# Attention weights read back from DRAM by groups of 32 partitions: one change to a hybrid encoder block

## The chip, the cores and the metric

The kernel runs on one core of a Trainium2 chip. The metric is the device time of one execution in microseconds (us). Three runs of the kernel before took 1124.34, 1127.92 and 1130.77 us; their median is 1127.92 us.

## The reference

One encoder layer on 512 tokens of width 1024, in float32. It has a half-step feed-forward block, a mixer, and a second half-step feed-forward block. The mixer runs two branches on one normalised input and merges them with two sigmoid gates. Branch A is a convolution with two gated linear recurrences. Branch B, which the change touches, is neighbourhood attention over a grid of 8 rows and 64 columns with 16 heads of width 64:

```
x = x + 1/2 * SwiGLU_1(RMSNorm(x))
h = RMSNorm(x);  xr, gr, q, k, v, ga, gb = split(h @ W_in)
A = (rglru_forward(conv(xr)) + rglru_backward(conv(xr))) * gelu(gr)
q, k = RMSNorm per head
s = q . k over an 8 x 16 window + bias[head, drow, dcol]
B = softmax(s) @ v
x = x + (sigmoid(ga) * A + sigmoid(gb) * B) @ W_out
x = x + 1/2 * SwiGLU_2(RMSNorm(x))
```

## The kernel before

**Matmuls.** Every float32 matmul on weights is made of three: each operand is split into a high and a low part (`split`, ScalarE writes the high part, VectorE the low part), and high x high, high x low and low x high are summed. The weights of one chunk (`wraw`, 512 KB) are loaded by SyncE's queue, split into `wh` and `wl`, and used by 24 matmuls over 512 tokens. There are three `wraw` buffers and four pairs `wh`, `wl`, so the split of a later chunk waits until TensorE is done with an earlier one.

**Attention.** The 16 heads are handled in two halves (`hf` 0 and 1) of four head pairs each (`fi` 0 to 3; a pair is two heads of 64 on 128 partitions). The 512 tokens are in four column blocks `n` of 128 queries; a pair of column blocks is `n2`. In the first half TensorE turns q and k; in the second VectorE turns them in 32 x 32 blocks, and they go through DRAM (`qd`, `xqk`). For each head pair:

- `start` makes the high and low parts of q and k (`qh`, `ql`, `kh`, `kl`; lines 944 to 969).
- `scores` multiplies q and k (line 988), and makes the softmax: `so` adds the bias `bm` and takes the minimum of the negated sum on VectorE (line 1008), ScalarE makes the exponentials `p` (line 1015), VectorE the reciprocal `rs` (1017), ScalarE scales `p` (1020).
- `ship` turns the weights. With queries on partitions, `p` holds keys in columns. VectorE transposes 32 x 32 blocks into `pt` (lines 1029 and 1030), SyncE's queue stores `pt` to DRAM (`pd`, line 1032), and four loads by GpSimd's queue bring it back as `PT` with keys on partitions (line 1036). A PT has 128 partitions of four groups `j` of 896 bytes; group `j` holds the queries of one 32-partition block of `pt`.
- `apply` multiplies v by `PT` (line 1051) and ScalarE evicts it to `att` (1061). It reads all of a `PT`.

There are 16 such blocks, two for each head pair, called PT 1 to PT 16 here. `PT` has five buffers, `pd` four, `pt` two.

**Order.** The heads are written as generators and woven into the gate matmuls (`gates`, line 1113; matmuls at lines 172 to 174, eviction at line 1119): after a number of gate matmuls that a table of rates sets, one more step of the attention is written. `apply` of a head pair is written two pairs behind its scores in the second half (`ATT_LAG`), the last two at the end. A scheduler then orders each engine's instructions by its own estimates, and inserts the waits. Each engine runs its instructions in that order.

**GpSimd's queue** issues, one after the other: the four loads of each PT, the biases `bm` (line 895), and v in the shapes that the column blocks need (`vs`, line 872; `va` and `ve`, line 883, read only by `apply`). The kernel is built with `dynamic_dma_scratch_size=2048`, the room for what GpSimd writes to have its DMAs carried out.

Of the kernel before, what the change touches and what calls it, by code (L numbers as in the profile page):

```python
# [91 lines left out]
def block_kernel(ctx: ExitStack, tc, a, out):  # L92
    nc = tc.nc
# [14 lines left out]
    def nm(s):  # L108
        uid[0] += 1
        return f"{s}_{uid[0]}"  # L110
# [147 lines left out]
    def sub(out_, in0, in1, neg=False):  # L258

        if neg:  # L260
            nc.vector.scalar_tensor_tensor(out_, in0, -1.0, in1, ALU.mult, ALU.subtract)
        else:
            nc.vector.tensor_tensor(out_, in0, in1, ALU.subtract)
# [672 lines left out]
    def heads(hf, raws, qd):  # L936
# [86 lines left out]
        def ship(fi, n2):  # L1023

            outer, inner = soft.pop((fi, n2))
            t = big.tile([P, NCB, 7, 32], F32, tag="pt", bufs=2, name=nm("pt"))
            sub = lambda b, n: b[:, : n * P].rearrange("p (q c i) -> p q c i", q=n, i=32)
            to = t.rearrange("p c q i -> p q c i")
            nc.vector.transpose(to[:, 4:], sub(outer, 3))
            nc.vector.transpose(to[:, :4], sub(inner, 4))  # L1030
            d = dram.tile([P, NCB, 7 * 32], F32, tag="pd", bufs=4, name=nm("pd"))
            nc.sync.dma_start(d, t.rearrange("p c q i -> p c (q i)"))
            PT = big.tile([P, NCB, 7, 32], F32, tag="PT", bufs=5, name=nm("PT"))
            for j in range(4):
                q = slice(j * 32, (j + 1) * 32)
                nc.gpsimd.dma_start(PT[:, j].rearrange("p q i -> p (q i)"), d[q].rearrange("i c x -> c i x"))  # L1036
            PTs[fi, n2] = PT.rearrange("p a q i -> p q a i")

        def apply(fi, behind=None):
# [31 lines left out]
        for i, (fi, n2s) in enumerate(units):  # L1071
            behind = scores(fi, n2s)
            if i >= LC and 1 in units[i - LC][1]:
                apply(units[i - LC][0], behind)
            for n2 in n2s:
                ship(fi, n2)
            if 0 in n2s:
                if fi < 3:
                    start(fi + 1)
                if hf * 4 + fi + 1 < KT:  # L1080
                    bias(hf * 4 + fi + 1)
            if phase[0] == "g":
                yield
                if hf == 1:
                    yield
            yield
# [170 lines left out]
```

## Time and profile before

| | |
|---|---|
| median of three runs | 1127.92 us |
| profiled execution | 1128.13 us, span 1126.4 us |
| TensorE busy | 1100.3 us, 98% of the span |
| VectorE, ScalarE, GpSimd busy | 796.3, 619.5, 148.4 us |
| packets of GpSimd's DMA queue | 20752, 46.80 MB |
| PT loads | 64 of 112 KB, median 4.9 us from issue to landing |

Times in the trace are counted from the start of the span. Engines: PE is TensorE, DVE VectorE, ACT ScalarE, POOL GpSimd, SP SyncE. A row of the timeline gives start, duration, engine, line, operation, names out<-in, and in brackets the idle time before it with what ended it. "issue" means that the engine waited for nothing that the profile shows. Buffer numbers are left out of names in the profile and kept in the order listings.

### The profile page before, as it was taken

How to read it: one execution, taken by the hardware profiler on the slowest of the kernel's cores; microseconds unless marked ns; L12 is line 12 of the kernel's file. 1: busy time of each engine (PE TensorE's matmuls, PEld its weight loads, DVE VectorE, ACT ScalarE, POOL GpSimd, SP SyncE). 2: the span in 40 equal slices, each digit the busy share in tenths (PEclk: the TensorE clock that was granted, in tenths of full speed). 3: DMA queues.
4: the chain of work that ended last, by engine and by line, in shares of the span. 5: the costliest groups of instructions: out<-in, count | busy, mean ns of one | idle time of the engine just before them, and what ended most of it. 6: DMA issues, size and time to landing. Idle time of an engine off the chain costs nothing.

```text
span 1126.4 us, 17668 instructions
## 1 busy us (share of the span) xinstructions
PE 1100.3 (98%) x6779; PEld 974.1 (86%) x6779; DVE 796.3 (71%) x1228; ACT 619.5 (55%) x950; POOL 148.4 (13%) x243
## 2 busy tenths in 40 slices
PE   9999999999999999999999598999999999999998
PEld 8899999988888778787887476888999999998887
DVE  7877777785836877998875562768877877784642
ACT  8554545553624778877777462446645454464330
POOL 0000000000000441241234531000000000000000
PEclk9999999999999999999999799999999999999999
DMA  7566666643423784754798674377666666663321
GB/s 264 153 165 153 168 147 155 173 138 98 131 80 103 199 239 137 200 175 131 259 275 210 190 193 123 94 225 186 174 164 168 152 147 157 165 168 94 130 76 38
DMA packets 73571, 180.12 MB, mean 160 GB/s; under 512 B 23056, under 2 KB 26896, under 8 KB 73488
## 3 DMA queue, kind: packets, MB, share of 16 engines
q1 hardware_dynamic: 52160, 131.94, 36.4%
q0 software_dynamic: 20752, 46.80, 20.8%
q8 instruction: 53, 0.87, 0.3%
q10 hardware_dynamic: 576, 0.26, 0.1%
q14 instruction: 30, 0.25, 0.1%
HBM read 152.63 MB, written 17.83 MB: 151 GB/s over the span
## 4 chain that ended last, share of the span: by engine, by line
PE 90%; issue 3%; DMA 2%; POOL 2%; ACT 1%; DVE 1%; SPq 0%; POOLq 0%; ACTq 0%; DVEq 0%
PE acc L312 31%; PE acc L172 9%; PE acc L173 9%; PE acc L174 9%; PE aux L312 5%; PE acc L834 4%; PE acc L835 4%; PE acc L836 4%; PE aux L172 4%; PE aux L173 4%; PE aux L174 4%; POOL PT L1036 1%; DMA PT<-pd 1%; PE aux L742 1%; PE aux L1051 1%
## 5 line engine op out<-in xcount | busy, mean ns | idle before, releaser
L145 ACT ACTIVATE wh<-wraw 128x1024 fp32r<-128x1024 f32 (+3 forms) x236 | 233.4, 991 | 321.0 <-issue 88.5
L148 DVE TENSOR_TENSOR wl<-wraw,wh 128x1024 fp32r<-128x1024 f32 (+3 forms) x236 | 267.5, 1136 | 99.9 <-ACT wh L145 96.4
L312 PE MATMUL acc<-s,wh 128*128 128x256 f32 x1280 | 232.2, 283 | 0.0
L312 PEld LDWEIGHTS acc<-s,wh 128*128 128x128 f32 x1280 | 199.7, 192 | 0.0
L312 PE MATMUL acc<-s,wl 128*128 128x256 f32 x640 | 181.1, 283 | 0.0
L312 PEld LDWEIGHTS acc<-s,wl 128*128 128x128 f32 x640 | 122.9, 192 | 0.0
L172 PE MATMUL acc<-xh,wh 128*128 128x512 f32 x272 | 107.8, 396 | 0.0
L174 PE MATMUL acc<-xh,wl 128*128 128x512 f32 x272 | 106.5, 392 | 0.0
L173 PE MATMUL acc<-xl,wh 128*128 128x512 f32 x272 | 106.2, 391 | 0.0
L312 PE MATMUL acc<-xh,wl 128*128 128x256 f32 x320 | 90.6, 283 | 0.0
L312 PE MATMUL acc<-xl,wh 128*128 128x256 f32 x320 | 90.6, 283 | 0.0
L312 PE MATMUL acc<-xh,wh 128*128 128x256 f32 x320 | 90.5, 283 | 0.0
L834 PE MATMUL acc<-wh,xh 128*128 128x512 f32 x192 | 75.7, 394 | 1.0 <-ACT qk L846 1.0
L148 DVE TENSOR_TENSOR hl<-h,hh 128x512 fp32r<-128x512 f32 x88 | 57.3, 686 | 25.4 <-PE aux L173 24.3
L835 PE MATMUL acc<-wh,xl 128*128 128x512 f32 x192 | 74.8, 389 | 0.0
L836 PE MATMUL acc<-wl,xh 128*128 128x512 f32 x192 | 74.7, 389 | 0.0
L172 PE MATMUL aux<-hh,wh 128*128 128x512 f32 (+1 forms) x181 | 69.9, 386 | 0.0
L173 PE MATMUL aux<-hl,wh 128*128 128x512 f32 (+1 forms) x181 | 69.9, 386 | 0.0
L174 PE MATMUL aux<-hh,wl 128*128 128x512 f32 (+1 forms) x181 | 69.9, 386 | 0.0
L173 PE MATMUL acc<-hl,wh 128*128 128x512 f32 (+1 forms) x176 | 67.9, 386 | 0.0
L174 PE MATMUL acc<-hh,wl 128*128 128x512 f32 (+1 forms) x176 | 67.9, 386 | 0.0
L172 PE MATMUL acc<-hh,wh 128*128 128x512 f32 (+1 forms) x176 | 67.9, 386 | 0.0
(226 smaller groups left out, 2304.1 us busy)
## 6 DMA issues: line engine op xcount, KB each, us to landing
wraw<-wqkv SPq DMA_DIRECT2D x24, 512.0 KB
wraw<-wg SPq DMA_DIRECT2D x24, 512.0 KB
wraw<-w1d SPq DMA_DIRECT2D x22, 512.0 KB
wraw<-w2s SPq DMA_DIRECT2D x22, 512.0 KB
pair<-w2s SPq DMA_DIRECT2D x22, 512.0 KB
wraw<-w2d SPq DMA_DIRECT2D x22, 512.0 KB
wraw<-w1s SPq DMA_DIRECT2D x18, 512.0 KB
pair<-w1s SPq DMA_DIRECT2D x18, 512.0 KB
```

The costliest lines, as they stand in the source:

```text
L145: nc.scalar.activation(H, raw, AF.Copy)
L148: return nc.vector.tensor_tensor(L, raw, H.bitcast(F32), ALU.subtract)
L172: nc.tensor.matmul(ps, wh, xh, start=first, stop=False, skip_group_check=skip)
L173: nc.tensor.matmul(ps, wh, xl, start=False, stop=False, skip_group_check=skip)
L174: mark["mm"] = nc.tensor.matmul(ps, wl, xh, start=False, stop=last, skip_group_check=skip)
L312: mm = nc.tensor.matmul(o, w_[:, c], x_, start=first and m + k == 0 and w_ is H and x_ is xh_, stop=m + k == 4 and w_ is L, skip_group_che ...
L742: prev, mm = mm, nc.tensor.matmul(ps[d][b], W[w][o, c], X[x][o], start=x == 1, stop=w + x == 0)
L834: nc.tensor.matmul(pss[j], xh[kk][:, tj], H[:, s], start=kk == 0, stop=False)
L835: nc.tensor.matmul(pss[j], xl[kk][:, tj], H[:, s], start=False, stop=False)
L836: mark["mm"] = nc.tensor.matmul(pss[j], xh[kk][:, tj], L[:, s], start=False, stop=kk == KT - 1)
L1036: nc.gpsimd.dma_start(PT[:, j].rearrange("p q i -> p (q i)"), d[q].rearrange("i c x -> c i x"))
L1051: mm = nc.tensor.matmul(pv[h2 * HD : (h2 + 1) * HD, n * P : (n + 1) * P], vt[:, (fi * 2 + h2) * HD : (fi * 2 + h2 + 1) * HD], PT[:, q], st ...
```

## The change

The four loads of a PT are cut another way. Before, load `j` wrote group `j` of all 128 partitions, from 32 rows of `pd` that lie one behind the other. Now load `c` writes the 32 partitions of key block `c`, all four groups of them, from one 896-byte piece of each of the 128 rows of `pd`. The number of loads, their bytes and the length of the contiguous pieces are the same, and so is the data in `PT`.

```
             PT = big.tile([P, NCB, 7, 32], F32, tag="PT", bufs=5, name=nm("PT"))
-            for j in range(4):
-                q = slice(j * 32, (j + 1) * 32)
-                nc.gpsimd.dma_start(PT[:, j].rearrange("p q i -> p (q i)"), d[q].rearrange("i c x -> c i x"))
+            for c in range(4):
+                q = slice(c * 32, (c + 1) * 32)
+                nc.gpsimd.dma_start(PT[q].rearrange("p j q i -> p j (q i)"), d.rearrange("(j i) c x -> c i j x", j=4)[c])
             PTs[fi, n2] = PT.rearrange("p a q i -> p q a i")
```

In the built program a load's counts, from the outermost dimension, go from 128 x 1 x 224 on the tile's side and 4 x 32 x 224 in DRAM to 32 x 4 x 224 on both sides. The change applies to both halves of the heads. The scheduler's order moves as well, from about the second head pair of the second half on; the places that count are shown in the prediction.

## The prediction, made before the result was known

> **What bounds the kernel now.** I read the slices of the page first, then the idle times of TensorE in its timeline, then what the releasers of those waits waited for themselves.
>
> ```profile
> PE 1100.3 (98%) x6779; PEld 974.1 (86%) x6779; DVE 796.3 (71%) x1228; ACT 619.5 (55%) x950; POOL 148.4 (13%) x243
> PE   9999999999999999999999598999999999999998
> PEclk9999999999999999999999799999999999999999
> ```
>
> TensorE works without a break except in the 23rd and 25th slice, where the granted clock dips too; a slice is 28.2 us, so that is from about 620 us on, and by the timeline 606 to 696 us. Only this stretch has time to give. Its idle times in the timeline of PE (idle and releaser in brackets):
>
> ```profile
> 608.21 0.39 PE L988 MATMUL aux<-kl,qh 64*128 64x256 f32 x2 [1.47 <-DVE kl L965]
> 630.38 0.39 PE L988 MATMUL aux<-kl,qh 64*128 64x256 f32 x2 [4.52 <-DVE kl L965]
> 633.21 0.70 PE L1051 MATMUL aux<-PT,va 128*64 128x128 f32 x4 [0.43 <-DMA PT<-pd]
> 638.82 1.12 PE L1051 MATMUL aux<-PT,vs 128*64 128x128 f32 x8 [3.92 <-DMA PT<-pd]
> 641.75 0.69 PE L1051 MATMUL aux<-PT,va 128*64 128x128 f32 x2 [1.81 <-DMA va<-vd]
> 644.72 0.45 PE L1051 MATMUL aux<-PT,va 128*64 128x128 f32 x1 [2.29 <-DMA va<-vd]
> 664.24 0.66 PE L1051 MATMUL aux<-PT,vs 128*64 128x128 f32 x8 [1.71 <-DMA PT<-pd]
> 692.66 1.12 PE L1051 MATMUL aux<-PT,vs 128*64 128x128 f32 x8 [4.02 <-DMA PT<-pd]
> ```
>
> They add up to 20.2 us, 14.2 of it on transfers that POOL issues (PT, va). After the long ones the clock is halved for a while (windows: length, PE busy, ..., PEclk):
>
> ```profile
> 631.10:634.40 3.30, 2.87 (x30) 2.60 (x28) 3.30 (x14) 1.36 (x6) 1.02 (x2) 0.50 0.94 179
> 638.00:648.00 10.00, 5.09 (x38) 3.98 (x40) 0.49 (x1) 0.60 (x1) 7.10 (x10) 0.50 0.55 155
> 692.60:695.80 3.20, 3.14 (x19) 2.62 (x20) 0.00 (x0) 0.60 (x1) 0.00 (x0) 0.50 0.03 5
> ```
>
> 2.87 + 5.09 + 3.14 = 11.1 us of matmuls at half clock, of which half, 5.5 us, is lost. The stretch costs 25.7 us in all.
>
> Why the transfers are late stands in POOL's waits and its timeline:
>
> ```profile
> POOL PT L1036 <- issue: 64.7, 30, 6.3
> 526.66 2.03 POOL L1036 DMA_DIRECT2D PT<-pd  x3 [24.53 <-DMA pd<-pt]
> 530.60 0.66 POOL L1036 DMA_DIRECT2D PT<-pd  x1 [1.90 <-issue]
> 610.82 0.59 POOL L895 DMA_DIRECT2D bm<-rpb  x1
> 614.36 0.70 POOL L1036 DMA_DIRECT2D PT<-pd  x1 [2.94 <-issue]
> 618.55 0.66 POOL L1036 DMA_DIRECT2D PT<-pd  x1 [0.86 <-issue]
> 619.20 1.16 POOL L895 DMA_DIRECT2D bm<-rpb  x2
> 617.61 0.36 DVE L1008 CUSTOM_DVE_ANT_0 so<-aux,bm 128x192 f32<-128x192 f32 x1 [7.66 <-DMA bm<-rpb]
> DMA to landing us min/median/max: 3.6/4.9/10.5
> ```
>
> Each block needs four PT loads. Three go out back to back, and the fourth stalls in its own issue until the first has landed (526.66 + 3.6 = 530.3, issue at 530.60): three PT loads in flight fit somewhere, four don't. At 618.55 to 619.20 two bm loads, 128 rows each as well, pass with PT loads in flight and no stall. So a PT load takes much more of what is full. What it takes is seen where queue q0 carries three PT loads alone (packets and issues of 540 to 545.2 us):
>
> ```profile
> DMA packets 631, 1.25 MB, mean 241 GB/s; under 512 B 328, under 2 KB 337, under 8 KB 631
> q0 software_dynamic: 375, 0.33, 25.9%
> PT<-pd POOLq DMA_DIRECT2D x3, 112.0 KB, 4.4
> ```
>
> No row of a PT load is under 896 B, yet about 296 of q0's 375 packets are under 512 B (the other 32 of the 328 are completions of two transfers on q1). Per load that is 125 packets, near 16 rings of 8: 4 rings with 32 rows each (packets of five rows and one of two, the 9 between 512 B and 2 KB), 12 rings with padding of the same length, and a completion on each. I read: the rows go over 4 engines, and every ring is charged 32 entries and a completion, 33 in all. Three loads are 99; four would be 132.
>
> **The change part by part.** Issues, bytes and row size stay: 64 loads of 128 rows of 896 B. What changes is the pair of leading counts: 128 on the tile's side against 4 in DRAM before, 32 against 32 now. A bm load, 128 against 128, has no padding. By that row 32 against 32 spreads over 16 engines with 8 rows and a completion each, 9 entries; the other end is that it stays at 33. I take 9, since nothing in the new shape has a 4 in front. [...]
>
> Then four loads take 36 entries, POOL issues a block in 4 x 0.67 = 2.7 us, and what is queued behind (bm, va) goes out at once. The scheduler reorders as well, in three places that matter. POOL, between the last block of the first half (PT_6059) and the first two of the second (PT_6236, PT_6246):
>
> ```order
> +L1036 DMA PT_6059<-pd_6057 32x4x224 x4
>  L895 DMA bm_6266<-rpb 128x640
> -L1036 DMA PT_6059<-pd_6057 128x1x224 x4
>  L895 DMA bm_6462<-rpb 128x640
>  L895 DMA bm_6464<-rpb 128x640
> -L1036 DMA PT_6236<-pd_6234 128x1x224 x4
> +L1036 DMA PT_6236<-pd_6234 32x4x224 x4
> +L1036 DMA PT_6246<-pd_6244 32x4x224 x4
>  L879 MEMSET ve_6269 128x512
> ```
>
> bm_6266, for which DVE waited until 617.61, now stands behind a whole block of loads. DVE, ahead of the second head pair's softmax (so_6393):
>
> ```order
>  L965 TENSOR_TENSOR kl_6254<-xqk_6144,kh_6253 128x4x8x16
>  L148 TENSOR_TENSOR wl_6716<-wraw_6714,wh_6715 128x1024
> +L1119 TENSOR_TENSOR pair_6476<-acc_6478,rstd_3727 128x512
> +L148 TENSOR_TENSOR wl_6756<-wraw_6754,wh_6755 128x1024
>  L1008 ISA so_6393,nmx_6394<-aux_6361,bm_6264 128x192
> ```
>
> The softmax now waits for a gate chunk of 24 matmuls (acc_6478) that PE starts after the scores. And DVE, ahead of the third pair's scores, which need kl_6452:
>
> ```order
> -L148 TENSOR_TENSOR wl_6756<-wraw_6754,wh_6755 128x1024
> +L962 SCALAR_TENSOR_TENSOR ql_6450<-xqk_6259,gq_3677,qh_6449 128x4x128
> +L1119 TENSOR_TENSOR pair_6477<-acc_6542,rstd_3727 128x512
> +L148 TENSOR_TENSOR wl_6928<-wraw_6926,wh_6927 128x1024
> +L965 TENSOR_TENSOR kl_6452<-xqk_6259,kh_6451 128x4x8x16
>  L1017 RECIPROCAL rs_6360<-rs_6360 128x2
> ```
>
> kl_6452 moves ahead of the transposes, but behind the eviction of chunk acc_6542, all of whose 24 matmuls now precede the scores (21 before). The walk uses these rows:
>
> ```profile
> 609.89 0.50 PE L172 MATMUL acc<-xh,wh 128*128 128x512 f32 x1
> 625.47 0.39 PE L174 MATMUL acc<-xh,wl 128*128 128x512 f32 x1
> L148 DVE TENSOR_TENSOR wl<-wraw,wh 128x1024 fp32r<-128x1024 f32 x11 | 13.4, 1214 | 0.9 <-ACT wh L145 0.9
> L145 ACT ACTIVATE wh<-wraw 128x1024 fp32r<-128x1024 f32 x11 | 11.6, 1056 | 16.4 <-PE acc L173 15.1 <-DMA wraw<-wg 1.3
> L1119 DVE TENSOR_TENSOR pair<-acc,rstd 128x512 f32<-128x512 f32 x11 | 7.5, 684 | 32.3 <-PE acc L174 32.2
> L965 DVE TENSOR_TENSOR kl<-xqk,kh 128x512 fp32r<-128x512 f32 x3 | 2.0, 683 | 0.0
> 682.31 1.99 POOL L1036 DMA_DIRECT2D PT<-pd  x3 [3.59 <-DMA pd<-pt]
> 674.87 0.33 SPq L1032 DMA_DIRECT2D pd<-pt  x1
> ```
>
> First the scores at 608.21: they wait for an eviction and a kl after the last gate matmul, 0.68 + 0.68 and a hand-over, 1.47. Order and wait stay. From 609.89 to 625.47 there are 69 gate matmuls, 0.229 us apart, so a chunk of 24 lasts 5.5 us. Chunk acc_6478 ends near 615.5; the split of the next weights (1.06 on ACT, whose buffer that chunk frees, 1.21 on DVE) ends near 617.8, and the softmax starts there, as late as the 617.61 of now; bm_6266 has room if POOL no longer stalls. SP is reordered too: the store of this pair's first block (pd_6432) stands behind two weight loads whose buffer comes free with the split near 623.4, about when its transposes end; that costs 1 us at most, and the block is wanted 25 us later. Chunk acc_6542 ends at 609.89 + 72 x 0.229 + 0.2 = 626.5. Behind it come wh 1.06 on ACT, wl 1.21 and kl 0.68 on DVE with their hand-overs, 3.1 us, and the scores start at 629.6. This wait is 3.1 instead of 4.52. Is the clock halved behind it? The idle times of 1.71 and 1.47 were not followed by half clock, those of 3.92 and more were; 3.1 is nearer to 3.92, so I take one dip of 3.4 us, 1.7 lost, with 0 as the other end.
>
> From there: two applies (PV products) without a wait, 48 gate matmuls, then the fourth pair's scores. Their kl also stands behind an eviction now (kl_6672 behind that of acc_6753, whose last four matmuls move ahead of the scores): again 0.68 + 0.68, 1.47 us, where the kl was ready before. Then apply, 48 gates, apply, 36 gates, the last apply. The blocks have room: by my walk PT 12 lands about 5 us before its apply, PT 14 some 7. The tight one is PT 16. Its store went out at 674.87, 15 us after the scores, and took 7.4 us to 682.3. With the fourth scores at 648, softmax and transposes of 10 us (nothing between them waits for a chunk now), a store of 7.4, an issue of 2.7 and 4 us to land give 672; its first product is due near 674. I cost it at 0, with 4 us as the other end.
>
> **The sum.** Before: 20.2 + 5.5 = 25.7. After: 1.47 + 3.1 + 1.47 idle and 1.7 for the clock, 7.7. Gain 18.0. PE is busy without a break from 696 us to the end, so the gain reaches the end. The profiled execution took 1128.13 us with a span of 1126.4; the median of the runs is 1127.92. 1128.13 - 18.0 = 1110.1; I forecast **1110 us**. Its own range: 1108 without the clock dip, 1116 with PT 16 late by 4 us and a dip behind it.
>
> **The rivals.** *Late landings.* Each load now writes into 32 partitions only. If it then lands as late as the loads did in the busiest stretch (maximum 10.5, median 4.9), the tight block comes 5.6 - 2 = 3.6 us late, with another dip, 1.7, and one or two of the earlier waits stay in part, 2 to 4: 1110 + 7 to 9, about 1118. For it: 32 x 896 B x 4 in a quarter of the tile. Against: xqk loads of the same grouping hold up nobody on PE. [...]
>
> *The ring stays full, slower.* If a load still takes 33 entries (the scheduler keeps its new order all the same), bm_6266 stands behind the block whose fourth load went out at 618.55. It goes at 619.2 and lands with the bm median of 6.3 at 625.5, not 617.5:
>
> ```profile
> DMA to landing us min/median/max: 3.8/6.3/8.8
> ```
>
> The second softmax, kl_6452 and all behind slip by up to 8 us, of which 3 lie under the gates; the waits for PT stay. 1128 + 5 = 1133. 99 entries are seen to fit, so it cannot decide below 25 entries a load.
>
> *No change.* POOL's stall goes, but the blocks were late for another reason, the stores on SP and the chunk-locked DVE, and the waits come back elsewhere. Against: 64.7 us of POOL's idle time is its own issue, and block 16's store waited for nothing but its transposes. 1127.
>
> **How the numbers follow.** Relief as walked 0.67, late landings 0.17, no change 0.08, slower 0.08. A difference of 0.5%, 5.6 us, is about what a measurement tells from none. Faster 0.84, same 0.08, slower 0.08. The range for all, 1104 to 1119, takes in the first two cases and, below, a walk that overrates the two kl waits and the dip by most of their 6 us.
>
> **What would show it.** In the page, q0 falls from 20752 packets by 64 x (128 - 48) = 5120 to about 15632 (16 x 3 per load in place of 16 x 8). That settles the engines by itself. POOL's timeline shows PT x4 in one row, its waits on issue for PT fall from 64.7 to a few us, DVE's wait for bm is gone. PE keeps three idle times, near 1.5, 3.1 and 1.5 us, all for kl, and none for PT or va but perhaps the last; PEclk dips at most once. Wrong it would be if q0 keeps its packets, or if PE waits for kl for more than 8 us in all.
>
> ```profile
> q0 software_dynamic: 20752, 46.80, 20.8%
> ```

## The result, and the profile after

The changed kernel took 1109.04 us, the median of four runs (1108.49 to 1109.71), beside 1127.82 us for the kernel before in the same comparison (1124.34 to 1130.77, four runs). The ratio is 0.9835, with a 95% interval of 0.9806 to 0.9864, so 15 to 22 us were gained. The profiled execution took 1108.49 us with a span of 1106.7 us.

The page of the changed kernel, the rows that answer those of before (busy times, slices, clock, GpSimd's queue):

```profile
PE 1093.7 (99%) x6779; PEld 969.0 (88%) x6779; DVE 796.1 (72%) x1228; ACT 619.1 (56%) x950; POOL 140.1 (13%) x243
PE   9999999999999999999999899999999999999998
PEclk9999999999999999999999999999999999999999
q0 software_dynamic: 15632, 46.70, 21.5%
```

The hole in the 23rd and 25th slice is gone but for one 8, and so is the dip of the clock. The queue's packets are 15632, 48 a load in place of 128, to the packet the number forecast. The span fell by 19.7 us: 6.6 us of TensorE's busy time (1100.3 to 1093.7; 5.5 of them are the prediction's half clock, 5.7 by the exact windows of the last section; the rest is not traced) and 13.1 us of its idle time (1126.4 - 1100.3 = 26.1 before, 1106.7 - 1093.7 = 13.0 now). The waits left in the attention stretch, in TensorE's timeline:

```profile
559.54 0.44 PE L1051 MATMUL aux<-PT,va 128*64 128x128 f32 x4 [1.26 <-DVE ql L962]
609.56 0.38 PE L988 MATMUL aux<-kl,qh 64*128 64x256 f32 x2 [1.48 <-DVE kl L965]
630.63 0.38 PE L988 MATMUL aux<-kl,qh 64*128 64x256 f32 x2 [2.78 <-DVE kl L965]
648.61 0.39 PE L988 MATMUL aux<-kl,qh 64*128 64x256 f32 x2 [1.47 <-DVE kl L965]
```

No wait is on a transfer any more. Three are the predicted ones for `kl`; the first, 1.26 us, wasn't predicted. The profiled execution is the fastest of the four and has full clock throughout; the other three took 0.5 to 1.2 us more at a granted clock of 0.998 in place of 1.000. GpSimd's waits on its own issue (total, times, longest), two pieces of its timeline, and the landings of PT:

```profile
POOL va L883 <- issue: 12.1, 7, 3.3
POOL ve L883 <- issue: 6.2, 4, 2.0
POOL PT L1036 <- issue: 0.2, 1, 0.2
615.59 2.18 POOL L1036 DMA_DIRECT2D PT<-pd  x4 [6.07 <-DMA pd<-pt]
661.97 2.26 POOL L1036 DMA_DIRECT2D PT<-pd  x4 [1.22 <-DMA pd<-pt]
DMA to landing us min/median/max: 2.6/5.4/8.0
```

The 64.7 us of stalls on PT are 0.2. Four loads go out in one row; what GpSimd waits for ahead of them is the store (`pd<-pt`), not room. The median landing is 5.4 us, 4.9 before; the shortest is 2.6 instead of 3.6 and the longest 8.0 instead of 10.5. The medians are not like for like, as four loads are now in flight at once and before it was three.

### The profile page after: what moved, and what is told of

It reads as the page before. It is cut to its first block, busy times and chain, and to the rows that moved or that the text cites. A ratio compares the mean times of both kernels' runs of the same rounds, so it can differ in the third digit from the quotient of the medians.

```text
span 1106.7 us, 17673 instructions
## 1 busy us (share of the span) xinstructions
PE 1093.7 (99%) x6779; PEld 969.0 (88%) x6779; DVE 796.1 (72%) x1228; ACT 619.1 (56%) x950; POOL 140.1 (13%) x243
## 3 DMA queue, kind: packets, MB, share of 16 engines
q0 software_dynamic: 15632, 46.70, 21.5%
## 4 chain that ended last, share of the span: by engine, by line
PE 95%; DMA 1%; DVE 1%; ACT 1%; issue 1%; SPq 0%; ACTq 0%; DVEq 0%
PE acc L312 31%; PE acc L172 11%; PE acc L173 10%; PE acc L174 10%; PE aux L312 5%; PE acc L834 4%; PE aux L172 4%; PE aux L174 4%; PE aux L173 4%; PE acc L835 4%; PE acc L836 4%; PE aux L1051 1%; PE aux L742 1%; PE aux L988 1%; DMA vd<-v 1%
```

## The experiments

The rivals for the gain: room for entries in GpSimd's queue (the theory), the scheduler's new order, the narrow shape of 32 partitions, and the larger number of engines as such. Each comparison had its own runs of the kernel before, with medians of 1127.82 to 1130.07 us.

**The kernel before with more room, and with less.** The order of all engines stays as before.

```
-dynamic_dma_scratch_size=2048
+dynamic_dma_scratch_size=3072      (and 1024)
```

> The kernel before, with 3072 in place of 2048 bytes of scratch for GpSimd's DMAs, nothing else; every engine's order stays. Theory of the ring (a PT load takes 33 entries a ring, 2048 bytes hold 128 of them, so 3072 hold 192 and five loads fit): the fourth load of a block no longer stalls, PT x4 in one row of POOL's timeline, POOL's waits on issue for PT fall from 64.7 us to under 15, and most of the gain comes without the change: 1108 to 1116 us. Rival of the engines (the gain is that the rows go over 16 engines and land sooner): loads still on 4 engines, 1125 to 1130 us. Rival of the order (the gain is the scheduler's new order): 1125 to 1130 us.

> The kernel before, with 1024 bytes, same order. Theory of the ring: 64 entries, a second load of 33 never fits, so each PT load waits until the one before has landed: 64 x 4.9 us is 314 us of POOL's time in place of some 165 now (525 to 690 us), and va and ve go one at a time too. TensorE waits for blocks: 1220 to 1290 us. Rivals of the engines and of the order: 1125 to 1130 us.

With 3072 it took 1112.51 us (1108.82 to 1113.47), ratio 0.9859 (0.9836 to 0.9882). GpSimd's waits, the landings of PT and TensorE's waits for transfers in that kernel:

```profile
POOL PT L1036 <- issue: 15.4, 12, 3.5
DMA to landing us min/median/max: 3.5/6.0/11.3
630.50 0.43 PE L1051 MATMUL aux<-PT,va 128*64 128x128 f32 x2 [0.77 <-DMA va<-vd]
633.08 0.29 PE L1051 MATMUL aux<-PT,va 128*64 128x128 f32 x1 [2.14 <-DMA va<-vd]
674.82 0.66 PE L1051 MATMUL aux<-PT,vs 128*64 128x128 f32 x8 [1.21 <-DMA PT<-pd]
```

Room alone, without one changed load and in the old order, brings nearly all of the gain; its interval overlaps that of the change. The loads are cut there as before (20752 packets, by the prediction's reading over 4 engines), so neither more engines nor the new order are needed. The stalls on PT fell from 64.7 to 15.4 us, just over the 15 expected. The trace is of its execution of 1108.82 us, at a clock of 1.000.

With 1024 it took 1295.04 us (one run), 5 us above the range expected. TensorE's waits, and GpSimd's timeline at the first blocks:

```profile
PE aux L1051 <- DMA PT<-pd: 128.4, 11, 17.4
532.20 0.69 POOL L1036 DMA_DIRECT2D PT<-pd  x1 [2.10 <-issue]
538.22 0.69 POOL L1036 DMA_DIRECT2D PT<-pd  x1 [5.33 <-issue]
```

Each load goes out alone, after a wait of 2.10 and 5.33 us in its issue. What fits at 2048 can be bounded from the traces of the kernel before and of the changed one. Reckoned with 33 entries for an old PT load, a `va` or a `ve` and 9 for any other, up to 117 entries are in flight in the first and up to 126 in the second, the load just issued among them. Of the stalls over 0.2 us that GpSimd has on the issue of PT, `va` and `ve`, 35 of 38 and 10 of 11 begin where the next load would bring 132 or more. In proportion to the size this gives, as an estimate, 63 to 66 entries at 1024 and 189 to 198 at 3072: one old load fits, or five. The traces show them one at a time at 1024, three in a row at 2048 (526.66 us) and four in a row at 3072 (640.77 us). The 64, 128 and 192 of the expectations lie within these bounds; that the room is exactly this isn't shown.

**The changed kernel with less and with more room.** Same one-number edit, same order as the changed kernel.

> The changed kernel with 1024 bytes in place of 2048, order as changed. Theory of the ring: four PT loads take 36 of 64 entries and still go without a stall; va and ve (33 each) go one at a time, about 3 us apiece for 12 in each half, mostly hidden: 1109 to 1119 us, q0 at 15632 packets. If the new loads took 33 entries after all, over 1220 us.

> The changed kernel with dynamic_dma_scratch_size=3072, all engines in the same order. Nothing of the computation is left out. Theory (with 9 entries a load the ring no longer bounds anything that PE waits for): GpSimd's waits on issue for va and ve, 18 us together, fall to less than 4, and the time stays at 1108 to 1110 us. Rival (what is left of the stalls, va and ve with 33 entries each, still costs PE's time): 1104 to 1107 us.

With 1024 it took 1127.04 us (1124.24 to 1129.15), ratio 0.9985 (0.9972 to 0.9998), no gain left: a miss by 8 us at the least. GpSimd's waits and TensorE's two longest:

```profile
POOL PT L1036 <- issue: 7.0, 8, 2.8
POOL va L883 <- issue: 38.6, 13, 4.9
POOL ve L883 <- issue: 26.4, 8, 5.4
634.41 0.58 PE L988 MATMUL aux<-kl,qh 64*128 64x256 f32 x2 [6.90 <-DVE kl L965]
648.14 0.44 PE L1051 MATMUL aux<-PT,va 128*64 128x128 f32 x1 [7.65 <-DMA va<-vd]
```

The PT loads go out in fours or threes even there (three at 617.09 and at 621.58 us), with 7.0 us of stalls. The loads of v, `va` and `ve` (64 rows of 4 pieces each), still take 33 entries, by the same reckoning, and go one at a time (635.15, 639.68, 642.55, 645.45 and 648.31 us). I had expected that, and about its price in stalls (12 in each half at 3 us, 72 us; found 65.0); what I had wrong is "mostly hidden". They hold up all that is behind them, and TensorE waits 7.65 us for a `va` itself. The same room for entries, then, with another payer.

With 3072 it took 1109.40 us (1107.60 to 1109.61), ratio 0.9820 (0.9797 to 0.9843), the time of the changed kernel:

```profile
POOL ve L883 <- issue: 6.3, 3, 3.2
POOL va L883 <- issue: 0.4, 1, 0.4
```

The stalls of `va` and `ve` fall from 18.3 to 6.7 us (not below 4 as expected) and TensorE gains nothing: what is left of them at 2048 is off its path.

**Which half's loads.** The new loads in one half of the heads, the old ones in the other (`hf == 0`, then `hf == 1`).

```
+if hf == 0:            # hf == 1 in the second kernel
     for c in range(4): ...   # loads by 32 partitions
+else:
+    for j in range(4): ...   # loads by group j, as before
```

> The new loads for PT 1 to 8 alone; PT 9 to 16 are loaded by key block as before, and PE, DVE and SP keep the order of before. Nothing of the computation is left out. Theory (room for entries): q0 falls by half, to 20752 - 32 x 80 = 18192 packets. GpSimd's waits on issue for PT fall to about half of 64.7 us; the backlog of the first half is gone, so bm comes in time, DVE's wait of 7.66 us goes, and of PE's waits the 4.52 for kl and the clock dip behind it; the stalls of the second half stay and with them 1.7 + 4.0 us for PT and the dip of 1.6 behind 692 us. So half to two thirds of the gain of 18.8 us: 1116 to 1121 us. Rival (the new order makes the gain): no gain, about 1128 us. Second rival (the first half's stalls do no harm, since PE waited only after 606 us): 1126 to 1128 us.

> The new loads for PT 9 to 16 alone; PT 1 to 8 are loaded by key block as before, and PE and DVE have the order of the changed kernel. Nothing of the computation is left out. Theory (room for entries): 18192 packets on q0; the stalls around PT 7 and PT 8 stay (bm goes out late, 618 to 619 us, and kl is late with it, 4 to 5 us of PE's idle time with a clock dip of 1.7), PE waits for no PT after 650 us: 1113 to 1118 us. Rival (the new order makes the gain): 1109 us. Second rival (only the second half counts): 1109 to 1111 us. With this the gains of the two halves are to be compared: more than 19 us together means that either alone removes part of the same waits.

("By key block as before" in these two means the old loads, by group `j`.)

The first half alone: 1116.41 us (1115.38 to 1116.71), ratio 0.9878 (0.9858 to 0.9899), in the range expected. It has the order of before on TensorE and VectorE, so the order isn't what gains. Both kernels have 18192 packets. What it has left, GpSimd's waits and TensorE's timeline:

```profile
POOL PT L1041 <- issue: 32.2, 18, 5.7
633.57 0.29 PE L1056 MATMUL aux<-PT,va 128*64 128x128 f32 x1 [2.86 <-DMA va<-vd]
679.92 1.12 PE L1056 MATMUL aux<-PT,vs 128*64 128x128 f32 x8 [3.99 <-DMA PT<-pd]
```

The second half alone: 1121.55 us (1116.52 to 1122.36), ratio 0.9916 (0.9887 to 0.9946). That is slower than the 1113 to 1118 expected (one of its four executions, 1116.52, lies within), and the rival of the order, 1109, falls: this kernel has the new order on TensorE and VectorE and keeps less than half of the gain.

```profile
611.71 0.66 POOL L1041 DMA_DIRECT2D PT<-pd  x1 [6.83 <-issue]
635.24 0.69 PE L1056 MATMUL aux<-PT,va 128*64 128x128 f32 x4 [3.35 <-DMA PT<-pd]
640.26 1.12 PE L1056 MATMUL aux<-PT,vs 128*64 128x128 f32 x8 [3.05 <-DMA PT<-pd]
644.91 0.44 PE L1056 MATMUL aux<-PT,va 128*64 128x128 f32 x1 [2.64 <-DMA va<-vd]
```

The miss: I had charged the old loads of the first half with a late bias only. A single old load stalls for 6.83 us there, behind it the next blocks and `va` go out late, and the applies of 632 to 645 us wait for them; the clock is halved for 20.5 us, 629.7 to 650.1 by the spacing of the matmuls (mean granted clock 0.991 of 1120.6 us), in which some 11.2 us of matmuls ran, so that 5.6 us are lost. The half clock begins behind the wait of 2.78 us for `kl`, which the changed kernel has too; here TensorE was busy 0.6 us in the 3.41 us ahead of it. It lasts through the waits for PT and `va`. By the medians the backlog of the first half is the larger part of the loss. The gains, 13.7 and 8.5 us, add up to 22.2, more than the 18.8 of the whole change, but within their intervals; that both remove some of the same waits stays likely and unproved.

**Sixteen engines without the narrow shape.** The store is cut in four and laid out so that a load by group `j` reads 128 contiguous rows.

```
-d = dram.tile([P, NCB, 7 * 32], ...);  nc.sync.dma_start(d, t...)
+d = dram.tile([4, NCB, 32, 7 * 32], ...)
+for j in range(4):
+    nc.sync.dma_start(d[j].rearrange("c i x -> i c x"), t[j * 32 : (j + 1) * 32]...)
 for j in range(4):
-    nc.gpsimd.dma_start(PT[:, j]..., d[q].rearrange("i c x -> c i x"))
+    nc.gpsimd.dma_start(PT[:, j]..., d[j].rearrange("c i x -> (c i) x"))
```

> Loads by key group j of 128 partitions again, as in the kernel before, but the store to DRAM is cut in four on SyncE's queue and laid out so that the 128 rows of each load lie one behind the other: leading counts 128 on both sides, 16 engines, without the narrow shape of 32 partitions. Nothing of the computation is left out. The scheduler orders all engines anew with the three more stores a block. Theory (the number of engines and entries counts, not which partitions a load writes): q0 15632 packets, no stall of a fourth PT load, no wait of PE for PT, 1106 to 1114 us; the three more stores a block (4 instead of 1 on SyncE's queue) can cost up to 3 us. Rival (it is the grouping by 32 partitions that helps): waits for PT stay, 1122 to 1130 us.

It took 1118.60 us (1116.97 to 1118.94), ratio 0.9897 (0.9876 to 0.9918), outside both ranges. Its queue, GpSimd's wait for PT, TensorE's only long wait, and part of SyncE's queue there:

```profile
q0 software_dynamic: 15632, 46.70, 20.6%
POOL PT L1036 <- issue: 1.8, 8, 0.5
615.43 0.79 PE L172 MATMUL acc<-xh,wh 128*128 128x512 f32 x1 [12.98 <-ACT wh L145]
600.38 5.62 SPq L1033 DMA_DIRECT2D pd<-pt  x8
608.33 11.59 SPq L163 DMA_DIRECT2D wraw<-wg  x5
```

What the theory says of the loads holds: the packets, no stall, and no wait of TensorE for a PT. So the grouping by 32 partitions as such isn't what helps; a load that covers 128 partitions in 48 packets does too. The loads of that kernel also land sooner, 2.2 us at the least and 4.2 in the median, beside 2.6 and 5.4 for those of 32 partitions. The price of the stores was mis-sized. I had put 3 us on SyncE's queue, for more stores in it; what cost the time, by this trace, is the order that the scheduler gave that queue. Between 555 and 608 us it issues no load of gate weights, where the changed kernel issues seven; the last eight stores stand at 600.38 to 606.0 ahead of them, the loads start at 608.33, and TensorE, out of split weights, waits 12.98 us for one.

**The waits for kl.** First the predicted new waits were tried by undoing what places `qh` and `kh` in the order: no `hold` (an order behind the last gate matmul) in the second half.

```
-hold(nc.scalar.activation(k_of(kh), xk, AF.Copy))
+keep = hold if hf == 0 else lambda i: i      # the same for qh
+keep(nc.scalar.activation(k_of(kh), xk, AF.Copy))
```

> The changed kernel without the rule that puts the q and k parts of the second half (lines 960 and 963) behind the gate matmuls written before them. Three waits of TensorE for kl are left after the change (1.5, 2.8 and 1.5 us). Theory: they come from DVE's order, kl behind the eviction of a chunk that ends just before the scores; if kl moves ahead of that eviction they go: 1103 to 1106 us. Rival: the scheduler moves more than kl, and the waits come back elsewhere: 1107 to 1115 us.

It took 1109.16 us (1108.68 to 1110.12), ratio 0.9838 (0.9820 to 0.9857), as the changed kernel.

```profile
608.73 0.39 PE L989 MATMUL aux<-kl,qh 64*128 64x256 f32 x2 [0.70 <-DVE kl L966]
630.89 0.40 PE L989 MATMUL aux<-kl,qh 64*128 64x256 f32 x2 [3.85 <-DVE kl L966]
```

The first wait is halved and the third gone, the second grew to 3.85 and half clock follows (the scores' matmuls 0.21 us apart, 0.12 before; mean granted clock 0.998): the rival holds, what is won at one place is lost at the other. Then the place itself, VectorE's evictions of gate chunks ahead of `kl`, was changed:

```
-nc.vector.tensor_tensor(q[i // 2][:, i % 2], ps, rb, ALU.mult)
+ev = nc.vector.tensor_tensor(q[i // 2][:, i % 2], ps, rb, ALU.mult)
+if phase[0] == "g" and "kl" in mark:
+    after(ev, mark["kl"])
```

> The changed kernel, in which VectorE's evictions of gate chunks in the attention stretch are ordered behind the last kl that was written before them, so that no kl stands behind an eviction. Nothing of the computation is left out. Reading of the changed kernel's trace: PE's three waits for kl, 1.48 + 2.78 + 1.47 = 5.7 us, come from that place in VectorE's order; without it the scores start at once: 1103 to 1106 us. Rival: the evictions that come later hold up the buffers of the next gate chunks, or the softmax and so a PT, and the waits come back in another place: 1108 to 1113 us.

TensorE keeps its order exactly. It took 1104.10 us (1103.63 to 1104.58), ratio 0.9771 (0.9747 to 0.9794), faster than the changed kernel: the intervals don't meet. VectorE's and TensorE's timelines:

```profile
625.64 0.69 DVE L965 TENSOR_TENSOR kl<-xqk,kh 128x512 fp32r<-128x512 f32 x1
626.25 1.28 DVE L1119 TENSOR_TENSOR pair<-acc,rstd 128x512 f32<-128x512 f32 x2
626.38 0.38 PE L988 MATMUL aux<-kl,qh 64*128 64x256 f32 x2
644.05 0.40 PE L988 MATMUL aux<-kl,qh 64*128 64x256 f32 x2 [1.02 <-DVE kl L965]
```

`kl` is done before the chunk ends and the scores start without a wait; of 5.7 us one wait of 1.02 is left. That VectorE's order was the cause of the three waits is shown by this, though ScalarE's order and one `memset` of GpSimd's moved along with it.

**The wait that wasn't predicted.** ScalarE's timeline, before:

```profile
553.53 0.51 ACT L1015 ACTIVATE p<-so,nmx 128x256 f32<-128x256 f32 x1 [0.55 <-DMA vd<-v]
```

and in the changed kernel:

```profile
555.11 0.51 ACT L1015 ACTIVATE p<-so,nmx 128x256 f32<-128x256 f32 x1 [2.12 <-DMA vd<-v]
```

An exponential waits 1.6 us longer for SyncE's stores of v, in whose buffer it writes; `ql` behind it is late, and TensorE with it. I read that PT 3's loads, no longer held back, share the engines with these stores, and wrote the loads of PT 3 behind the stores of v, with a wait for the last of them:

```
 for j in range(NCB):
-    nc.sync.dma_start(vd[hf][...], V[hf, 2 * j])
+    st = nc.sync.dma_start(vd[hf][...], V[hf, 2 * j])
+for load in mark.pop("late", []):      # PT 3's four loads, kept back by ship
+    after(load(), st, True)
```

> The changed kernel with the four loads of PT 3 written after the four stores of the second half's v and made to wait for the last of them; PE's order is unchanged, GpSimd loads PT 3 behind PT 4, and one bm load goes out 2 us earlier. Nothing of the computation is left out. Theory (PT 3's loads, no longer held back by the ring, share the DMA engines with the stores of v, and ScalarE's p waits for those stores): PE's wait of 1.26 us at 558 us shrinks to 0.6 us or less, ScalarE's p at 555.1 starts up to 1.6 us earlier; 1107.5 to 1109 us. Rival (the wait has another cause, such as the bm loads, or its place is only a matter of how executions differ): the wait stays at 1.0 to 1.5 us, 1109 us.

> The same edit on the kernel with kl ahead of the evictions, which took 1104.1 us and had PE's waits 0.97, 1.41 (at 558 us) and 1.02. Nothing of the computation is left out. Theory: the 1.41 us at 558 us falls to 0.6 us or less, 1102.5 to 1104 us. Rival: it stays, 1104 us.

On the changed kernel this took 1114.53 us (1114.20 to 1115.95), ratio 0.9868 (0.9841 to 0.9894); on the kernel with `kl` first, 1113.63 us (1113.27 to 1113.93), ratio 0.9861 (0.9838 to 0.9883). Both are slower than the kernels that they start from, by 5.5 and 9.5 us, and lie outside both expectations. In the first of the two:

```profile
554.76 0.51 ACT L1017 ACTIVATE p<-so,nmx 128x256 f32<-128x256 f32 x1 [1.82 <-DMA vd<-v]
559.20 0.44 PE L1058 MATMUL aux<-PT,va 128*64 128x128 f32 x4 [0.97 <-DVE ql L964]
598.09 0.58 PE L990 MATMUL aux<-kl,qh 64*128 64x256 f32 x2 [5.29 <-DVE kl L967]
```

The wait falls to 0.97 (0.94 in the other, from 1.41), not to 0.6 or less: PT 3's loads explain a quarter to a third of it. A `bm` load went out earlier in their place, so the rest may be its bytes; that stays open. That the wait comes with loads that are no longer held back has more for it in the other runs: this exponential waits 0.65 us where the first half has the old loads at 2048, and 1.48 us with the old loads at 3072. And VectorE's order moved, so that a `kl` came 5.29 us late at 598, more than the edit could have brought.

## Why the prediction was right, point by point

**The bound.** TensorE idle in one stretch, and the clock behind it: right, by the 13.1 and 5.5 us above.

**The cause, 33 entries a load on every ring.** Right that it is room: shown by the room alone (1112.51 us), by its shortage (1295.04), and by the packets of 20 bytes, 4608 before and none after. The number 33 is an estimate from packets; that the stalls fit it (132 or more in 35 of 38) is a second hand for it. At 1024 the trace has a load alone in its queue (from 532.2 us) and shows the reading packet by packet: 28 packets with the rows (24 of five rows, 4 of two), 84 of 20 or 8 bytes, which I read as 4-byte pieces in the same fives and twos, and 16 completions of 4 bytes. By that reading there are 32 rows on each of 4 rings and 32 pieces of padding on each of 12; the trace doesn't name the ring of a packet.

**Nine entries after.** Right, by the packets: 15632, and for each load 16 of five rows (4480 bytes), 16 of three (2688) and 16 of 4 bytes, which I read as 8 rows and a completion on each of 16 engines. GpSimd's issue got cheaper as well, 0.552 us instead of 0.67, 2.2 us a block and not 2.7.

**The new waits for kl.** Predicted 1.47, 3.1 and 1.47 us, found 1.48, 2.78 and 1.47. The place was right too (the evictions, 1104.10 us without it). The scores started at 630.63 and not 629.6: 1.26 us from the unpredicted wait, less the 0.3 by which I had overrated this one.

**The clock dip, 1.7 us.** None came in the profiled execution. In the other three one likely did: their clock of 0.998 is that of the profiled execution with 3072, which has one window of 3.4 us at half clock; no trace of them is on record. They took 0.5 to 1.2 us longer, not 1.7. I had gone by the length of the idle time, and that doesn't tell the two cases apart: 2.78 us was followed by full clock here and by half clock with 3072 (the last section).

**PT 16, costed at 0.** Right. Its loads went out from 661.97 to 664.2 and had landed at 669.4, by my walk 672; its first product started at 673.62, and TensorE didn't wait.

**What the walk missed.** The wait of 1.26 us at 559, in the first half, where I had looked for nothing because TensorE had no idle time there before. The sum was 7.7 us left over; found were 1.48 + 2.78 + 1.47 + 1.26 = 7.0. A dip too many, in that execution, and a wait too few nearly cancel; so close a sum is luck.

**The rivals.** Late landings: no, the longest is 8.0 us; beside the loads of 128 partitions in 48 packets those of 32 landed a little later: 2.6 us at the least where those took 2.2, 5.4 in the median where those took 4.2. Those read contiguous rows and had other traffic beside them, so the cause isn't shown. Full ring: no, by q0. No change: no; the waits did come back elsewhere, but with 7 us of 25.7. The order, which I had kept in every sum, isn't needed for the gain (1116.41 with the old one, 1112.51 with the old one and more room). The waits for `kl` are most of what is left, 5.7 of 7.0 us; two of the three, 4.3 us, came with the new order.

## What to carry to other kernels

Here GpSimd's loads stalled in their own issue, 64.7 us in all, and what stood behind them was late (VectorE waited 7.66 us for a bias): look for waits on "issue" in that queue and count the packets of one load against its rows. Here 100 of a load's 128 packets were shorter than a row; try another grouping of the access (32 x 4 on both sides gave 48 packets and 0.2 us of stalls), or give the queue more room, which here was worth nearly as much (1112.51 us beside 1109.04). What such an edit does to the order of the other engines should be read as a change of its own: here it left three waits of 5.7 us, two of them new, and one more order edge brought them down to 1.0.

## What the runs showed of the hardware that was not expected

**The same wait, with full clock behind it and with half clock.** The wait of 2.78 us was followed by full clock in the changed kernel and by half clock with 3072. In the kernel before the granted clock is half from 631.07 to 634.49 us, from 637.90 to 648.14 and from 692.51 to 695.93, with 11.5 us of matmuls in these stretches. The six changes lie 3.41, 3.41, 10.24, 44.37 and 3.41 us apart, 1, 1, 3, 13 and 1 times 3.41. Windows of that length, counted from the clock's first entry in the trace (6.43 us in the kernel before, 4.41 in the changed kernel; start and end, length, PE busy, ..., PEclk), in the changed kernel:

```profile
625.63:629.04 3.41, 2.21 (x10) 1.50 (x8) 2.44 (x9) 3.38 (x10) 2.68 (x4) 1.00 0.94 304
629.04:632.45 3.41, 1.82 (x26) 1.66 (x28) 3.41 (x7) 2.43 (x6) 1.84 (x4) 1.00 1.01 251
```

in the changed kernel with 3072:

```profile
626.68:630.09 3.41, 0.96 (x5) 0.46 (x3) 2.54 (x4) 3.39 (x8) 0.25 (x1) 1.00 0.86 317
630.09:633.50 3.41, 3.07 (x26) 2.85 (x28) 3.41 (x8) 1.18 (x3) 2.21 (x4) 0.50 0.86 213
```

in the kernel before:

```profile
624.25:627.66 3.41, 1.60 (x8) 0.98 (x6) 2.83 (x5) 2.79 (x5) 1.55 (x3) 1.00 0.70 246
627.66:631.07 3.41, 0.69 (x10) 0.69 (x12) 3.41 (x7) 1.21 (x3) 1.72 (x3) 1.00 0.96 271
```

and with the first half's loads alone:

```profile
631.91:635.32 3.41, 1.53 (x22) 1.32 (x24) 1.99 (x8) 2.93 (x9) 3.41 (x6) 1.00 0.68 189
635.32:638.73 3.41, 3.41 (x23) 2.88 (x20) 0.04 (x1) 0.11 (x2) 0.25 (x1) 0.50 0.87 237
```

Of these windows at full clock, those of 1.60, 1.82 and 2.21 us busy were followed by full clock, those of 0.69, 0.96 and 1.53 by half clock. At half clock, in the kernel before, windows of 0.69 and 1.12 us busy were followed by half clock again, those of 2.99, 3.27 and 3.41 by full clock. No other window of the profiled executions of the kernel before and of the changed one has it otherwise. The wait of 2.78 us lay across two windows in the changed kernel (2.21 and 1.82 busy), and full clock followed; with 3072 most of it lay in one (0.96 busy), and the half clock behind it cost some 1.5 us, half of the 3.07 busy there. That its place among the windows made the difference is my reading of these two executions.

**A load of the same bytes took more room.** An old load and a new one carry 112 KB each. Of the old ones, 128 packets each, three went out in a row at 2048; of the new ones, 48 packets each, four, and eight at 563.00 us in the first kernel with PT 3 late. I read the 84 packets of 20 or 8 bytes as entries that take room without bytes. With room alone, 16.7 us of time came back.

**The new loads landed a little sooner, and that isn't what gained.** With four loads in flight at once, the old loads took 6.0 us in the median and 3.5 at the least (the kernel before with 3072), the new ones 5.2 and 2.5 (the changed kernel with 3072). The kernel with the old loads had nearly all of the gain all the same (1112.51 us): what the new loads gained here is room.
